# Twelve columns of the second gate formed during the first feed-forward part, with the contraction on the partitions

## The chip, the cores and the metric

The kernel runs on one core of one Trainium2 chip. The metric is device microseconds (us) of one execution; the figure of a kernel is the median of several runs. The core has engines that each work through their own instructions in order: PE (matrix products), DVE (VectorE, elementwise work and reductions), ACT (ScalarE, copies and activations), POOL (GpSimd, here only an issuer of transfers) and SP (SyncE, the main issuer of transfers). Transfers between the chip's memory (HBM) and the on-chip memory (SBUF) run on 16 DMA engines that all queues share.

## The reference, cut to what matters

One decoder layer, 512 tokens of width 2048, everything in float32:

```python
mod_all = silu(c) @ w_ada + b_ada               # w_ada: 2048 x 12288
sh1, sc1, g1, sh2, sc2, g2 = split(mod_all, 6)  # six vectors of 2048
h = rms_norm(x, norm1_g) * (1 + sc1) + sh1
u = h @ w_in                                    # all projections
mixed = [rms_norm(conv(u)), rms_norm(attention(u))]
x = x + g1 * (mixed @ w_out)
h = rms_norm(x, norm2_g) * (1 + sc2) + sh2
x = x + g2 * (relu(h @ w_ff1) ** 2 @ w_ff2)
return rms_norm(x, normf_g)
```

The change concerns g2, the second gate. It is needed only when the second feed-forward product is added to x, which is late in the kernel. Its 2048 numbers are kept as 16 columns of 128 (one column is 128 numbers, one on each SBUF partition), columns 80 to 95 of a tile called mod. One column costs 1 MB of w_ada; the twelve of the change cost 12 MB.

## The kernel before, in words

A matrix product in float32 is made of three products of a faster type (fp32r): each operand is split into a high half (a copy on ACT) and a low half (a subtraction on DVE). The pairs are called wh and wl in the projection and at the attention's output, hl, kw, sg or gt in the feed-forward part, and tk for tokens. So each weight block of 512 KB costs a transfer, an ACT operation and a DVE operation of 128x1024 before PE can use all of it.

The kernel has three stages, and each is recorded first and then emitted by a planner (the class Order). The planner knows a cost for every operation, simulates the engines and the DMA engines, and writes out for every engine an order, in which the engine then works whatever really happens. At each point it takes the operation that could start earliest; among those that could start equally early, the one with the earliest due time, which is counted back from the PE work that needs it. For a transfer it reckons that the data move no sooner than 1.5 us after the issue, at 340 GB/s, and have landed 1.1 us after that (in Order.plan: `wire = max(wire, at + 1.5) + x.size / Order.RATE` and `end = wire + 1.1`). The projection and the attention stage are planned six times and the best plan is taken; the feed-forward stage is planned once.

The stages are these.

- **Projection.** The columns of mod are formed beside it. One column is formed by two transfers of 512 KB (wa) and two "dots" on DVE: a multiply-and-sum of 1024 products along the free dimension for each of 128 partitions, against a copy of silu(c) spread over all partitions (cs). The profile names a dot CUSTOM_DVE t<-wa,cs. The list `todo` holds the columns that are formed here, in the order g1, sc2 and sh2, and then the first of g2; `more_ada(1)` takes one at a time.
- **Attention**, with the output product of the convolution half (out_conv, blocks w_oc) as filling work. At its end, `late_ada(NATT, 4, nc.gpsimd)` forms eight columns of g2 with loads on POOL's queue, into four tiles used in turn, with dots against a copy of cs that is loaded again. Behind it stand the first two blocks of w_oa (wh, wl).
- **Feed-forward.** First the rest of the attention's output product: `late_ada(len(behind), 4, nc.sync)` forms the last four columns of g2, six more blocks of w_oa are split (hl), and then blocks of w_oa2 (kw and others). Then the first feed-forward part: `part(n)` and `results_of(p)` for the rounds p = 0 and 1, and `ff1(p)` for p = 2 to 31. A round loads four blocks of w_ff1 into a ring of six tiles (rw), forms two sums (sg) and seven split operands, and runs seven products of 24 matmuls (a Strassen scheme, named B1, U6, T5, B2, T7, B3, T4); its results are split and stored (g). Up to p = 28, two of the sums of a round are made by transfers that add (POOL's queue, w_f into rw and sg). The second feed-forward part reads them back, and uses g2 from its sixth pass on.

The tile `spare` (128x1024, called snap in the profile) holds first results of rounds 0 and 1 and is then idle until the second feed-forward part.

Because one helper records all operations, every row of the profile has the same line, L142; tiles tell the operations apart.

Of the kernel before, what the change touches and what calls it, by code (L numbers as in the profile page):

```python
# [12 lines left out]
AF = mybir.ActivationFunctionType  # L13
OP = mybir.AluOpType
AX = mybir.AxisListType

P = 128
T = 512
D = 2048
NK = D // P  # L20
# [11 lines left out]
NSIDE = 7  # L32
NWA = 8
NBANK = 6
NLATE = 12
NATT = 8
NWARM = 3
SLACK = 4.0
FAST = 378e3
# [1 line left out]
V_BADA, V_N1, V_CW, V_CB, V_GC, V_GA, V_N2, V_NF, V_C, V_ID, V_END = \  # L41
    0, 96, 112, 136, 144, 152, 160, 176, 192, 208, 336
C_COS, C_SIN, C_MASK, C_CMASK, C_ROW, C_END = 0, 512, 1024, 1152, 1280, 1281
M_SH1, M_SC1, M_G1, M_SH2, M_SC2, M_G2 = range(6)
W_A, W_F, W_V = 64, 128, 134


def weave(ap, m):

    names = " ".join("xyz"[:len(ap.shape) - 2])  # L50
    return ap.rearrange(f"p {names} (a b i) -> p {names} a i b", b=2, i=m)


def plainly(ap, m):
    names = " ".join("xyz"[:len(ap.shape) - 2])
    return ap.rearrange(f"p {names} (a i b) -> p {names} a i b", b=2, i=m)
# [256 lines left out]
def hybrid_layer(ctx: ExitStack, tc: tile.TileContext, a, out):  # L313
    nc = tc.nc
# [10 lines left out]
    def slot(dtype=F32, name="m"):  # L325
        return mainp.tile([P, SLOT], dtype, name=name, tag="m")
# [5 lines left out]
    nc = order = Order(tc, xs[0].tensor.tag, NMAIN, passes=6)  # L332
# [63 lines left out]
    vec = consts.tile([P, V_END], F32, name="vec")  # L396
# [15 lines left out]
    ones = consts.tile([P, P], F32, name="ones")  # L412
# [3 lines left out]
    mod = consts.tile([P, 96], F32, name="mod")  # L416
# [4 lines left out]
    sc = small.tile([P, NK], F32, name="sc", bufs=1)  # L421
# [37 lines left out]
                             start=True, stop=True)  # L459
        return row_bcast(bank, total[:, t0:t1], width, dst[:, t0 * P:t1 * P])  # L460

    def row_bcast(bank, total, width, dst, turned=False):
        n = total.shape[-1]
        rs = small.tile([P, NQ], F32, name="rs", bufs=3)[:, :n]
        nc.scalar.activation(rs, total, AF.Sqrt, scale=1.0 / width, bias=eps)
        nc.vector.reciprocal(rs, rs)
        ps = spread(bank, rs)
        if turned:
            nc.scalar.activation(plainly(dst, W_A), weave(ps[:, :n * P], W_A), AF.Copy)
        elif dst is not None:  # L470
            nc.scalar.activation(dst, ps[:, :n * P], AF.Copy)
        return ps

# [30 lines left out]
    total = bank()  # L504
# [30 lines left out]
    for i in range(4):  # L535
# [6 lines left out]
    part = {}  # L542
    todo = [M_G1 * NK + k for k in range(NK)] + [w * NK + k for k in range(NK) for w in (M_SC2, M_SH2)] \
        + [M_G2 * NK + k for k in range(NK - NLATE)]
    behind = [M_G2 * NK + k for k in range(NK - NLATE, NK)]
    rb = accum("rb")

    def tokens(k, r):
# [98 lines left out]
    w = weights(a["w_kv"][0])  # L647
# [72 lines left out]
    def other():  # L720
        return next(others)

    def late_ada(n, slots, queue):
        c2 = [pair(name="cs") for _ in range(2)]
        for i in range(2):
            nc.sync.dma_start(out=c2[i], in_=csd[i])
        wa = [slot(name="wa")[:, :1024] for _ in range(slots)]
        for k in range(n):
            m, acc = behind.pop(0), next(accs)
            for i in range(2):  # L730
                w = wa[(2 * k + i) % slots]
                queue.dma_start(out=w, in_=a["w_ada"][2 * m + i])
                dot(w, i, acc, m, c2, temp(name="dot").bitcast(BF16))

    def more_ada(n):
# [432 lines left out]
    while m < NK:  # L1168
        out_conv(m)
        m += 1  # L1170
    late_ada(NATT, 4, nc.gpsimd)
    oa = [weights(a["w_oa"][k]) for k in range(2)]
    order.emit()
    att.close()
# [77 lines left out]

    late_ada(len(behind), 4, nc.sync)
    x1d = [dram.tile([P, 2, 2, HT], F32, name=f"x1d{i}") for i in range(NK // 2)]
    sacc = accum()
    pm = [bankf() for _ in range(8)]
# [132 lines left out]
    def outcome(p, x, y, zv):  # L1391

        store = nc.sync if p >= 30 else nc.gpsimd
        z, v = zv
        sub(z[:, 0], x[:, 0], y[:, 1])
        sub(z[:, 1], y[:, 1], y[:, 0])
        sub(v[:, 0], z[:, 0], y[:, 0], OP.add)
        sub(v[:, 1], x[:, 1], v[:, 0])
        for src, idx in ((x, (B1, B2)), (z, (T5, T7)), (v, (U6, T4))):
            g = next(gt)  # L1400
            tsplit(g, src)
            for j in range(2):
                store.dma_start(out=gd[p // 4][idx[j]][p % 4 // 2][:, p % 2].bitcast(F32), in_=g[:, j].bitcast(F32))
        for j, dst in enumerate((gd[p // 4][B3], g12d) if p >= 28 else (gd[p // 4][B3],)):
            g = temp((P, 2, HT), F32R, name="g12") if j else next(gb)
            split(g, y[:, j])
            store.dma_start(out=dst[p % 4 // 2][:, p % 2].bitcast(F32), in_=g.bitcast(F32))
# [45 lines left out]
    stay = {8: 5, 9: 6, 10: 7, 12: 1, 13: 3}  # L1453
    made, results, firsts = {}, {}, {}
    spare = slot(name="snap")[:, :1024]

    def make(n):
        p, b = plan[n][:2]
# [9 lines left out]
    def results_of(p):  # L1468
        x, y, z, v = [temp((P, 2, HT)) for _ in range(4)]
        for u in range(2):  # L1470
            nc.scalar.activation(x[:, u], results[p, u][:, LO], AF.Relu)
            sub(y[:, 1 - u], firsts[p, u], results[p, u][:, HI], OP.add)
        nc.scalar.activation(x, x, AF.Square)
        nc.scalar.activation(y, y, AF.Relu)
        nc.scalar.activation(y, y, AF.Square)
        outcome(p, x, y, (z, v))

    def part(n):
        p, b, i, u, hf, first = plan[n]
# [23 lines left out]
            results_of({13: 1, 15: 0}[n])  # L1503
    for p in range(NP, 32):
        ff1(p)


    ngate = consts.tile([P, NK], F32, name="ngate")
# [186 lines left out]
def _layouts(np, x, c, w_ada, b_ada, norm1_g, w_in, conv_w, conv_b, cmp_pe_k, cmp_pe_v, cmp_w1_k,  # L1695
# [16 lines left out]
    xt = x[0].T.reshape(NK // 2, 2, P, T).transpose(0, 2, 1, 3)  # L1712
    d["xt"] = xt.reshape(NK // 2, P, 2, T // P, P)[..., _stored(np, W_A)].reshape(xt.shape)
    d["xr"] = xt.reshape(NK // 2, P, 2, 2, T // 2)[..., _in_turn(np, W_F)].reshape(xt.shape)
    d["w_ada"] = w_ada[0].T.reshape(96, P, 2, 1024).transpose(0, 2, 1, 3).reshape(192, P, 1024)
    d["vec"] = np.concatenate(
        [cols(b_ada), cols(norm1_g), cols(conv_w), cols(conv_b), cols(gnorm_conv_g), cols(gnorm_attn_g),
         cols(norm2_g), cols(normf_g), c[0].reshape(NK, P).T, np.eye(P, dtype=np.float32), cmp_pe_k[0].T, cmp_pe_v[0].T, cmp_w2_k[0][:P], cmp_w2_k[0][P:],
# [47 lines left out]
```

## Time and profile before

| | |
|---|---|
| runs | 2025.38, 2024.46, 2023.94 us; median 2024.46 |
| profiled execution, its own time | 2025.47 us |
| its span, first to last instruction | 2023.7 us |
| mean granted clock of PE | 0.991 |
| busy: PE, DVE, ACT, POOL | 98%, 89%, 51%, 9% of the span |
| projection, attention, feed-forward (by PE's first s and first pf matmul) | up to 510, up to 688, up to 2024 us |

How to read it: a row of a timeline has the start, the duration, the engine, the operation, the tile written and the tiles read, and the shape; "x3" means three merged operations, and a bracket holds the idle time of the engine just before and what ended it. A group row has the count, then the busy time in us and the mean in ns, then idle time. In the list of transfers stand the count, the size and the median time from issue to landing. "PE" is the matrix engine's matmuls, "PEld" the loading of its weights.

### The profile page before, as it was taken

Reading aid. Unit: us, or ns where it says so; the run is one execution under the profiler, and the core shown is the slowest. Engines: PE = TensorE matmul, PEld = TensorE weight load, DVE = VectorE, ACT = ScalarE, POOL = GpSimd, SP = SyncE. Lnnn points to the kernel's source line nnn. Section 1 sums busy time; section 2 is a strip of 40 time slices with the busy share of each in tenths; the row PEclk is TensorE's granted clock in tenths of the full one; section 3 lists DMA queues with packets and bytes.
Section 4 is the critical chain, followed back from the end, with each engine's and each line's share of the span. In section 5 each row is a group of like instructions: output and inputs, shape, how many; then the busy total and the mean of one; then the engine's idle time right before and its main releaser. Section 6 shows DMA issues by size and latency. Waiting matters only on the chain.

```text
span 2023.7 us, 37782 instructions
## 1 busy us (share of the span) xinstructions
PE 1979.9 (98%) x14930; PEld 1887.1 (93%) x14930; DVE 1799.1 (89%) x2639; ACT 1036.4 (51%) x1533; POOL 182.9 (9%) x304
## 2 busy tenths in 40 slices
PE   8999999999999889999999999999999999999997
PEld 6888888989888779999999999999999999999997
DVE  8999988888998777988888888888989999999998
ACT  5444343334677236766666666665543333344345
POOL 0000000000000100233223223211000000000010
PEclk9999999999999989999999999999999999999999
DMA  9897688886211873698898899878867457468572
GB/s 374 333 353 251 231 290 315 288 302 243 93 63 63 284 274 129 178 296 257 271 281 253 264 280 261 257 232 315 298 226 262 152 212 271 157 214 294 181 233 100
DMA packets 140929, 487.19 MB, mean 241 GB/s; under 512 B 16976, under 2 KB 21584, under 8 KB 140752
## 3 DMA queue, kind: packets, MB, share of 16 engines
q1 hardware_dynamic: 111056, 384.10, 52.6%
q0 software_dynamic: 29120, 99.63, 18.4%
q8 instruction: 117, 1.92, 0.4%
q10 hardware_dynamic: 576, 1.05, 0.1%
q14 instruction: 60, 0.49, 0.1%
HBM read 415.51 MB, written 69.21 MB: 240 GB/s over the span
## 4 chain that ended last, share of the span: by engine, by line
PE 83%; DVE 9%; DMA 4%; issue 2%; ACT 1%; DVEq 0%; SPq 0%; ACTq 0%; POOLq 0%
PE pf L142 56%; PE ps L142 21%; PE pw L142 2%; DVE hl L142 2%; DVE xt L142 2%; PE s L142 2%; DMA wa<-in_w_ada 2%; PE pv L142 1%; DVE t L142 1%; PE pt L142 1%; DVE sg L142 1%; DMA rw<-in_w_f 1%; DVE wl L142 1%; DMA raw<-in_cmp_w 1%; DMA sg<-in_w_f 0%
## 5 line engine op out<-in xcount | busy, mean ns | idle before, releaser
L142 PE MATMUL pf<-tk,hl 128*128 128x256 f32 x10656 | 1193.9, 275 | 5.1 <-DVE t L142 2.6
L142 PEld LDWEIGHTS pf<-tk,hl 128*128 128x128 f32 x10656 | 1191.5, 192 | 6.6 <-issue 4.3
L142 ACT ACTIVATE hl<-rw 128x1024 fp32r<-128x1024 f32 x264 | 280.5, 1062 | 334.3 <-PE pf L142 309.6
L142 DVE TENSOR_TENSOR hl<-rw,hl 128x1024 fp32r<-128x1024 f32 x264 | 322.9, 1224 | 43.2 <-ACT hl L142 42.9
L142 ACT ACTIVATE hl<-sg 128x1024 fp32r<-128x1024 f32 x183 | 194.7, 1065 | 222.2 <-PE pf L142 199.5
L142 ACT ACTIVATE wh<-raw 128x1024 fp32r<-128x1024 f32 (+1 forms) x106 | 112.3, 1060 | 227.2 <-PE ps L142 170.4
L142 DVE TENSOR_TENSOR hl<-sg,hl 128x1024 fp32r<-128x1024 f32 x153 | 187.3, 1226 | 31.8 <-ACT hl L142 30.8
L142 PE MATMUL ps<-h_m,wh 128*128 128x512 f32 x720 | 215.0, 380 | 0.0
L142 PE MATMUL ps<-h,wh 128*128 128x512 f32 x560 | 166.0, 383 | 3.4 <-ACT h L142 2.6
L142 PEld LDWEIGHTS ps<-h_m,wh 128*128 128x128 f32 x720 | 135.2, 189 | 18.5 <-DVE h_m L142 0.2
L142 DVE TENSOR_TENSOR wl<-raw,wh 128x1024 fp32r<-128x1024 f32 (+1 forms) x106 | 129.9, 1226 | 16.6 <-ACT wh L142 15.5
L142 DVE CUSTOM_DVE_ANT_0 t<-wa,cs,acc 128x1024 bf16<-128x1024 f32 x96 | 123.1, 1283 | 23.6 <-DMA wa<-in_w_ada 22.3
L142 DVE CUSTOM_DVE_ANT_0 t<-wa,cs,vec 128x1024 bf16<-128x1024 f32 x96 | 122.9, 1282 | 17.1 <-DMA wa<-in_w_ada 16.5
L142 PE MATMUL ps<-h_m,wl 128*128 128x512 f32 x360 | 136.8, 380 | 0.0
L142 PEld LDWEIGHTS ps<-h,wh 128*128 128x128 f32 x560 | 106.3, 191 | 20.3 <-ACT h L142 4.2
L142 DVE TENSOR_TENSOR sg<-sg,rw 128x1024 f32<-128x1024 f32 x92 | 112.7, 1225 | 2.1
L142 POOL DMA_DIRECT2D g<-gt x180 | 97.0, 550 | 119.0 <-issue 55.2
L142 PE MATMUL ps<-h,wl 128*128 128x512 f32 x280 | 103.2, 381 | 0.0
L142 DVE TENSOR_TENSOR xt<-xt,pf 128x512 f32<-128x512 f32 x128 | 85.8, 683 | 9.4 <-PE pf L142 9.2
L142 POOL DMA_DIRECT2D rw<-in_w_f x30 | 26.3, 876 | 658.3 <-DVE sg L142 658.3
L142 PE MATMUL pw<-mix,wh 128*128 128x512 f32 x256 | 82.2, 392 | 0.0
L142 PEld LDWEIGHTS ps<-h_m,wl 128*128 128x128 f32 x360 | 68.2, 189 | 9.2
(240 smaller groups left out, 2282.1 us busy)
## 6 DMA issues: line engine op xcount, KB each, us to landing
rw<-in_w_f SPq DMA_DIRECT2D x260, 512.0 KB, 4.8
wa<-in_w_ada SPq DMA_DIRECT2D x176, 512.0 KB, 6.4
tk<-g SPq DMA_DIRECT2D x114, 512.0 KB, 6.5
g<-gt POOLq DMA_DIRECT2D x180, 256.0 KB, 7.1
raw<-in_w_conv SPq DMA_DIRECT2D x32, 512.0 KB, 4.5
rw<-in_w_f POOLq DMA_DIRECT2D x30, 512.0 KB, 6.1
sg<-in_w_f POOLq DMA_DIRECT2D x30, 512.0 KB, 5.5
raw<-in_w_kv SPq DMA_DIRECT2D x16, 512.0 KB, 6.4
```

Of the source, the lines that this page charges most:

```text
L142: x.i, x.eng, x.call = len(self.nodes), eng, (lambda: real(*args, **kw))
```

## The change

All sixteen columns of g2 leave the projection's list. Four (the first) are formed by `late_ada` at the start of the feed-forward stage, as four were before. The other twelve are formed in another way during the first feed-forward part, and the call at the attention's end is gone.

The new way: w_ada's last 1536 columns are laid out as `w_gate`, 48 blocks of 256 KB in which the contraction index lies on the partitions. `gate_part(s)` loads block s into the first half of `spare` and runs two DVE operations of 128x256 on it: each multiplies 256 outputs by one column of silu(c) (sc) as a scalar per partition, and adds to a running sum gsum in the last quarter of `spare`. After eight blocks, sixteen columns of sc have been used, and two matmuls with a column of ones sum gsum over the partitions; one small DVE operation adds the bias and writes two columns of mod. So two columns of g2 take eight blocks, and twelve take 48. The loop over p calls two blocks a round from p = 3 to p = 26. There is one tile for the loads, so a load waits until both operations on the block before are done. The rest of the diff drops an argument of row_bcast that no call uses.

```diff
-NLATE = 12
-NATT = 8
+NLATE = 16
+NGATE = 12
...
-    behind = [M_G2 * NK + k for k in range(NK - NLATE, NK)]
+    behind = [M_G2 * NK + k for k in range(NK - NLATE, NK - NGATE)]
...
-    def late_ada(n, slots, queue):
+    def late_ada(n, slots):
...
-                queue.dma_start(out=w, in_=a["w_ada"][2 * m + i])
+                nc.sync.dma_start(out=w, in_=a["w_ada"][2 * m + i])
...
-    late_ada(NATT, 4, nc.gpsimd)
     oa = [weights(a["w_oa"][k]) for k in range(2)]
...
-    late_ada(len(behind), 4, nc.sync)
+    late_ada(len(behind), 4)
...
     spare = slot(name="snap")[:, :1024]
+    gsum = spare[:, 3 * HT:]
...
+    def gate_part(s):
+
+        n, b = s // 8, s % 8
+        nc.sync.dma_start(out=spare[:, :T], in_=a["w_gate"][s])
+        for j in range(2):
+            w, c = spare[:, j * HT:(j + 1) * HT], sc[:, 2 * b + j:2 * b + j + 1]
+            if b + j == 0:
+                nc.vector.tensor_scalar(gsum, w, c, None, op0=OP.mult)
+            else:
+                nc.vector.scalar_tensor_tensor(out=gsum, in0=w, scalar=c, in1=gsum, op0=OP.mult, op1=OP.add)
+        if b == 7:
+            total = bankf()
+            m = M_G2 * NK + NK - NGATE + 2 * n
+            with floating():
+                for i in range(2):
+                    nc.tensor.matmul(total[:, i:i + 1], gsum[:, i * P:(i + 1) * P], ones[:, 0:1], start=True, stop=True)
+                nc.vector.tensor_tensor(out=mod[:, m:m + 2], in0=total[:, :2],
+                                        in1=vec[:, V_BADA + m:V_BADA + m + 2], op=OP.add)
...
     for p in range(NP, 32):
         ff1(p)
+        for s in range(2 * (p - NP - 1), 2 * (p - NP)):
+            if 0 <= s < 4 * NGATE:
+                gate_part(s)
...
+    early = D * 6 - P * NGATE
+    d["w_ada"] = w_ada[0][:, :early].T.reshape(-1, P, 2, 1024).transpose(0, 2, 1, 3).reshape(-1, P, 1024)
+    d["w_gate"] = w_ada[0][:, early:].reshape(8, 2, P, -1, T // 2).transpose(3, 0, 2, 1, 4).reshape(-1, P, T)
```

More of the change, by code (lines that the diff above doesn't have):

```diff
@@ L460, in row_norm, with row_bcast @@
         return row_bcast(bank, total[:, t0:t1], width, dst[:, t0 * P:t1 * P])
-    def row_bcast(bank, total, width, dst, turned=False):
+    def row_bcast(bank, total, width, dst):
         n = total.shape[-1]
@@ L467, in row_bcast @@
         ps = spread(bank, rs)
-        if turned:
-            nc.scalar.activation(plainly(dst, W_A), weave(ps[:, :n * P], W_A), AF.Copy)
-        elif dst is not None:
+        if dst is not None:
             nc.scalar.activation(dst, ps[:, :n * P], AF.Copy)
@@ L1714, in _layouts @@
     d["xr"] = xt.reshape(NK // 2, P, 2, 2, T // 2)[..., _in_turn(np, W_F)].reshape(xt.shape)
-    d["w_ada"] = w_ada[0].T.reshape(96, P, 2, 1024).transpose(0, 2, 1, 3).reshape(192, P, 1024)
+    early = D * 6 - P * NGATE
+    d["w_ada"] = w_ada[0][:, :early].T.reshape(-1, P, 2, 1024).transpose(0, 2, 1, 3).reshape(-1, P, 1024)
+    d["w_gate"] = w_ada[0][:, early:].reshape(8, 2, P, -1, T // 2).transpose(3, 0, 2, 1, 4).reshape(-1, P, T)
     d["vec"] = np.concatenate(
```

## The prediction

> **What bounds the kernel now.** The page comes first: how much of the span the matrix engine (PE) is busy, and which chain of work ended last.
>
> ```profile
> span 2023.7 us, 37782 instructions
> PE 1979.9 (98%) x14930; PEld 1887.1 (93%) x14930; DVE 1799.1 (89%) x2639; ACT 1036.4 (51%) x1533; POOL 182.9 (9%) x304
> PE 83%; DVE 9%; DMA 4%; issue 2%; ACT 1%; DVEq 0%; SPq 0%; ACTq 0%; POOLq 0%
> ```
>
> PE is the bound: 43.8 us (2023.7 - 1979.9) are all the time in which it does nothing. So an edit pays only by taking some of those 43.8 us away, or by shortening matmuls that run at a low clock, and it costs where it makes PE wait or adds to PE. The profiled execution took 2025.47 us, 1.8 us more than its span and 1.0 us more than the median of the runs (2024.46). I make the sum against 2025.5 and take 1.0 off at the end.
>
> The second view is PE's own timeline, read for its gaps near the places that the change touches: the end of the projection, and the border between attention and feed-forward part.
>
> ```profile
> 511.68 0.90 PE L142 MATMUL s<-kslc,q 128*128 128x160 f32 x6 [1.46 <-ACT gates L142]
> 516.00 0.56 PE L142 MATMUL s<-kslc,q 128*128 128x160 f32 x3 [2.52 <-DVE pc L142]
> 687.74 0.59 PE L142 MATMUL pf<-mixa,wh 128*128 128x512 f32 x2
> 692.79 0.38 PE L142 MATMUL pf<-mixa,wh 128*128 128x512 f32 x1
> 693.01 0.38 PE L142 MATMUL pf<-mixa,wl 128*128 128x512 f32 x1
> 696.49 0.48 PE L142 MATMUL pf<-mixa,wl 128*128 128x512 f32 x1 [2.67 <-DVE wl L142]
> 715.39 5.06 PE L142 MATMUL pf<-mixa,hl 128*128 128x512 f32 x11 [11.77 <-DVE hl L142]
> ```
>
> The bracket is the idle time ahead of a group and what ended it. The border holds 2.67 + 11.77 = 14.44 us of the 43.8, the start of attention another 1.46 + 2.52 = 3.98. Who makes PE wait stands in the timelines of VectorE (DVE) and ScalarE (ACT) at that border:
>
> ```profile
> 687.73 1.06 ACT L142 ACTIVATE wh<-raw 128x1024 fp32r<-128x1024 f32 x1 [4.61 <-PE pw L142]
> 688.69 1.04 ACT L142 ACTIVATE hl<-rw 128x1024 fp32r<-128x1024 f32 x1
> 688.52 1.28 DVE L142 CUSTOM_DVE_ANT_0 t<-wa,cs,acc 128x1024 bf16<-128x1024 f32 x1 [3.89 <-DMA wa<-in_w_ada]
> 695.21 1.22 DVE L142 TENSOR_TENSOR wl<-raw,wh 128x1024 fp32r<-128x1024 f32 x1
> 696.46 7.74 DMA rw<-in_w_oa
> 712.90 1.28 DVE L142 CUSTOM_DVE_ANT_0 t<-wa,cs,acc 128x1024 bf16<-128x1024 f32 x1 [7.55 <-DMA wa<-in_w_ada]
> 714.11 3.49 DVE L142 TENSOR_TENSOR hl<-rw,hl 128x1024 fp32r<-128x1024 f32 x3
> ```
>
> The operations t<-wa,cs are the "dots" of the second gate, and DVE works in order. The high half of the second w_oa block (wh) is ready at 688.8, but its low half (wl) stands behind five dots and starts at 695.21: PE waits 2.67 us. The next three low halves (hl) stand behind the sixteenth dot, whose weights land at 712.9: PE waits 11.77 us. All sixteen belong to the call at the attention's end, which the change takes out.
>
> **The change part by part.**
>
> *Taken out at the border: sixteen dots, sixteen loads on POOL's queue, two loads of cs on SP's.* Beside the two gaps goes the low clock behind them:
>
> ```profile
> 690.00:700.00 10.00, 7.30 (x28) 5.50 (x27) 8.93 (x14) 0.00 (x0) 2.63 (x5) 0.88 0.77 251
> 700.00:710.00 10.00, 3.62 (x15) 2.76 (x13) 2.59 (x4) 2.11 (x2) 0.53 (x1) 0.84 1.02 415
> 710.00:720.00 10.00, 4.61 (x11) 3.67 (x12) 7.06 (x8) 0.00 (x0) 0.00 (x0) 0.50 0.61 221
> 720.00:730.00 10.00, 10.00 (x45) 8.64 (x44) 1.92 (x4) 2.69 (x3) 0.00 (x0) 0.93 0.75 286
> ```
>
> Columns are PE, weight load, DVE, ACT and POOL busy, then granted clock, DMA share and GB/s. Busy time times the missing clock: 7.30 x 0.12 + 3.62 x 0.16 + 4.61 x 0.50 + 10 x 0.07 = 4.5 us. Gaps and clock are 14.4 + 4.5 = 18.9 us. (The Trainium skill, TensorE: Matmul & The Clock Gate, "What's actually happening", has the clock halved after an idle window of about 3.4 us. By it the gap of 2.67 us would cost no clock, and this term would be about 1.5 us smaller. The windows show a clock of 0.88 and 0.84 behind that gap, so the trace disagrees and decides.)
>
> What is late next there? Without the dots wl can end at 688.8 + 1.2 = 690.0. The loads of the fourth and later w_oa blocks, which follow wl, then start near 690 in place of 696.46; with the same 7.7 us they land at 697.7, and ACT (1.06) and DVE (about 1.2) make them ready at 700. PE, from 687.74 with 24 matmuls per block at 0.22 us (692.79 to 693.01), 5.3 us a block, wants the fourth at 703.6: 3.6 us to spare. The four columns that stay behind have their loads on SP behind these six. I take the whole 18.9; the low end is 7, if a load or one of the eight dots that stay takes the place of the large gap.
>
> *Taken out in the projection: four columns, eight dots and eight loads.* They are the last ones in the queue there:
>
> ```profile
> 491.50 1.28 DVE L142 CUSTOM_DVE_ANT_0 t<-wa,cs,acc 128x1024 bf16<-128x1024 f32 x1
> ...
> 496.91 1.29 DVE L142 CUSTOM_DVE_ANT_0 t<-wa,cs,acc 128x1024 bf16<-128x1024 f32 x1
> 512.13 2.51 DVE L142 SCALAR_TENSOR_TENSOR q<-t,q 128x512 fp32r<-128x512 f32 x4
> 515.00:520.00 5.00, 4.00 (x16) 3.29 (x17) 3.94 (x22) 3.01 (x12) 0.00 (x0) 0.66 0.07 25
> 520.00:525.00 5.00, 5.00 (x23) 4.40 (x24) 2.85 (x12) 2.09 (x8) 0.00 (x0) 0.66 0.00 0
> ```
>
> DVE runs without a pause into the first attention block and ends its q at 514.6; three of the eight dots, 3.9 us, lie in that run. Taking them out brings attention's start forward by up to 3.9 us, and up to 9.00 x 0.34 = 3.1 us of clock with it: 7.0 at most. The whole projection and attention are ordered anew by the planner, which can lose what it wins; I put the low end at -3, as much as the smaller of these terms. I take 4.0, the two gaps.
>
> *Added to PE: twelve column sums, each a matmul of 128x1 in f32.* The trace has this form:
>
> ```profile
> 384.23 1.05 PE L142 MATMUL ps<-ones,sacc 128*128 128x1 f32 x8 [0.70 <-DVE sacc L142]
> 385.14 0.36 PE L142 MATMUL ps<-wh,h 128*128 128x268 f32 x1
> L142 PE MATMUL pf<-ones,sacc 128*128 128x1 f32 x16 | 2.2, 243 | 0.2 <-DVE sacc L142 0.2
> ```
>
> Four of them hold PE from 384.23 to 385.14, 0.23 us each: 12 x 0.23 = 2.7 us. The other group gives 0.14 per record, 1.7 us, as the low end. PE has no gap in that stage (next fence), so this is paid in full.
>
> *Added to DVE and the DMA engines in the first feed-forward part: 48 loads of 256 KB on SP's queue, and behind each two operations of 128x256.* The twenty-four rounds p = 3 to 26, on which they are spread, take 450 us:
>
> ```profile
> 882.00:1332.00 450.00, 450.00 (x4032) 450.00 (x4031) 389.29 (x531) 290.72 (x410) 133.16 (x216) 1.00 0.90 268
> 1350.00:1400.00 50.00, 50.00 (x450) 50.00 (x449) 47.33 (x64) 29.82 (x43) 7.50 (x14) 1.00 0.74 254
> L142 DVE TENSOR_TENSOR t<-t 128x256 f32<-128x256 f32 x95 | 40.0, 421 | 0.0
> L142 DVE SCALAR_TENSOR_TENSOR x<-pf,mod,x 128x256 f32<-128x256 f32 x16 | 7.3, 480 | 6.1 <-PE pf L142 6.1
> rw<-in_w_f SPq DMA_DIRECT2D x96, 512.0 KB, 6.0
> g<-gb POOLq DMA_DIRECT2D x24, 256.0 KB, 5.3
> x<-in_xr SPq DMA_DIRECT2D x15, 256.0 KB, 4.5
> ```
>
> A round is 450 / 24 = 18.75 us. DVE is busy 389.29 / 24 = 16.22 of them and idle 2.53. Two steps a round are four operations of 0.42 us, 1.68: 0.85 us is left (0.61 if an operation takes 0.48). DVE would be at 95%, and in 1350 to 1400 it is at 47.33 of 50 beside a PE at 50.00, so the work by itself is hidden. The DMA engines are idle for 0.10 x 450 = 45 us; 48 x 0.262 MB at the 415 GB/s that they reach in 700 to 710 are 30 us. That fits too, if closely.
>
> What is not hidden by this is waiting. There is one tile, so a load waits for DVE's second operation on the load before, and DVE's next operation waits for the landing with every hl of the stage queued behind it. SP's weight loads stand behind the gate's load, but are issued well ahead. The planner reckons a 256 KB load at 1.5 + 0.77 + 1.1 = 3.4 us (constants in its code) and places DVE's operation from then on. The nearest rows say 4.5 us (same queue and size, quiet engines), 5.3 (same size, this stage, POOL's queue) and 6.0 (same queue and stage, twice the size). DVE's waits come in one cluster a round; here are the first and the last wait over 0.3 us of one round and the first of the next:
>
> ```profile
> 1020.56 0.42 DVE L142 TENSOR_TENSOR t<-pf,t 128x256 f32<-128x256 f32 x1 [0.43 <-PE pf L142]
> ...
> 1024.27 1.23 DVE L142 TENSOR_TENSOR hl<-sg,hl 128x1024 fp32r<-128x1024 f32 x1 [0.61 <-ACT hl L142]
> ...
> 1039.32 0.42 DVE L142 TENSOR_TENSOR t<-pf,t 128x256 f32<-128x256 f32 x1 [0.42 <-PE pf L142]
> ```
>
> The gate's operations come last in due time and so fall into these 4 us; one load of the two is then met tightly, and the other lands during the long busy stretch. With 4.5 us the wait is 1.1, less the free 0.85: 0.25 us x 24 = 6 us. With 3.4 it is 0; with 6.0, 2.6 - 0.85 = 1.75 x 24 = 42 us. I take the 4.5 row because size and queue are those of the gate's load.
>
> Sum: 2025.5 - 18.9 - 4.0 + 2.7 + 6 = 2011.3 for a profiled execution, **2010 us** for the median.
>
> **The rivals.**
>
> *The gate's loads land late all through the first feed-forward part, and DVE becomes the bound.* Place: rounds 3 to 26. With a landing of 5.5 us, between the rows of this stage, a round costs 16.22 + 1.68 + 2.1 = 20.0 us in place of 18.75, and 24 rounds 30 us: 2025.5 - 22.9 + 2.7 + 30 = 2035, median 2034, slower than before. It decides from the landing at which 24 x (wait - 0.85) exceeds the 20.2 us won, a wait of 1.7 us, a landing of 5.1. For it speaks a DMA share of 0.90 in that stage; against it that the dots of the projection, which meet the same planner in a busy stage, wait seldom:
>
> ```profile
> DVE t L142 <- DMA wa<-in_w_ada: 18.9, 17, 2.3
> ```
>
> That is 18.9 us in 17 waits between 200 and 500 us, the longest 2.3, though those loads have four tiles and the gate's has one. (The Trainium skill, DMA: Bandwidth & Descriptors, "Issuing engines are not separate DMA queues", speaks for this rival: transfers of SP and POOL share the same sixteen engines, so moving the loads from POOL's queue to SP's buys no room.)
>
> *The first feed-forward part hides everything.* The 256 KB loads land by the time that the planner reckons, or DVE comes late to each: the 6 us fall away, 2004 us. For it speaks that the planner gives the gate's operations the latest due time, so that any other ready operation goes first. (The Trainium skill, same page, "Anatomy of one DMA", puts a transfer at 2.0 us plus its bytes at 436 GB/s, an estimate of 2.6 us for 256 KB: by it every load is in time. The quiet 4.5 us row disagrees.)
>
> *The border keeps half its gap.* The eight dots that stay, or the loads of w_oa, hold the low halves up: the gain there is 7 to 12, the time 2017 to 2022. For it speaks that the dots that stay are ordered among the same hl operations; against it the 3.6 us to spare worked out above.
>
> **How the numbers follow.** Forecast (2006 to 2015) 0.45; all hidden (2000 to 2006) 0.17; half the gap stays (2015 to 2022) 0.18; DVE bound in the first feed-forward part (2022 to 2045) 0.20. The likeliest case's own range is 2006 to 2015. To leave out no more than 2 in 10, about one on each side, the range is 2001 to 2033: the low end has 7.0 from attention's start and nothing lost later, the high end nearly the price of the first rival. About 0.2% (4 us) is what a measurement of this kernel tells from no change, so faster means below 2020.4 and slower above 2028.5: faster 0.45 + 0.17 + 0.13 = 0.75; same 0.05 + 0.05 = 0.10; slower 0.15.
>
> **What would show it.** Border: no gap over 1 us on PE from its first pf matmul for 30 us, a granted clock of 1.00 there, and PE's first tk,hl matmul about 23 us earlier. Attention's start: no wait of s for DVE pc. First feed-forward part: DVE at 95% or a little more, waits of DVE for the load of w_gate of about 1 us once a round, a round of 19.0 us or less. Rounds of 19.6 us or more would make the prediction wrong; so would an hl that waits at the border for w_oa or w_ada.

## The result, and the profile after

The changed kernel takes 2042.85 us (median of 5 runs, 2036.48 to 2049.36) beside 2023.94 us (2022.89 to 2025.38) for the kernel before on the same chip. The ratio is 1.0095, with a 95% interval of 1.0068 to 1.0122. The change makes the kernel slower by 19 us where the forecast had it 14 us faster. The profiled execution took 2042.85 us, its span is 2041.0.

First the page of the changed kernel: span, busy times, the shares of the chain that ended last, and the last of the issues, the gate's loads.

```profile
span 2041.0 us, 37931 instructions
PE 1987.8 (97%) x14954; PEld 1893.1 (93%) x14954; DVE 1800.7 (88%) x2693; ACT 1034.3 (51%) x1533; POOL 175.2 (9%) x288
PE 76%; DVE 11%; DMA 8%; issue 3%; ACT 1%; DVEq 0%; SPq 0%; POOL 0%; ACTq 0%; POOLq 0%
snap<-in_w_gate SPq DMA_DIRECT2D x48, 256.0 KB, 4.9
```

PE's share of the chain has fallen from 83% to 76%, and that of the DMA engines has risen from 4% to 8%. PE's idle time is 2041.0 - 1987.8 = 53.2 us, 9.4 more than before. The rest of the 17.3 us between the spans is PE work: some at a low clock, some added.

PE's timeline from the end of the projection to the border, and a window of the border:

```profile
509.78 1.28 PE L142 MATMUL s<-kslc,q 128*128 128x160 f32 x9
680.59 0.60 PE L142 MATMUL pf<-mixa,wh 128*128 128x512 f32 x2
690.95 39.28 PE L142 MATMUL pf<-mixa,hl 128*128 128x512 f32 x216
690.00:700.00 10.00, 10.00 (x48) 8.76 (x47) 3.28 (x5) 1.06 (x1) 0.00 (x0) 1.00 1.03 417
765.91 2.84 PE L142 MATMUL pf<-tk,hl 128*128 128x256 f32 x24
```

The border does what was forecast: 216 matmuls of the low and high halves in one group without a bracket, the clock at 1.00, and the first tk,hl matmul at 765.91. In the trace of before it stands at 792.98, so 27.1 us are won by there: 687.74 - 680.59 = 7.1 by the first pf matmul, and 20.0 at the border.

All of that, and more, is lost again in the first feed-forward part. Its windows, and the waits between 800 and 1450 us:

```profile
820.00:1360.00 540.00, 513.91 (x4490) 508.87 (x4489) 460.96 (x691) 317.90 (x452) 147.92 (x239) 0.99 0.91 269
DVE snap L142 <- DMA snap<-in_w_gate: 39.8, 21, 4.5
PE pf L142 <- DVE snap L142: 16.0, 6, 4.5
PE pf L142 <- DVE t L142: 5.2, 8, 1.9
PE pf L142 <- DVE hl L142: 4.5, 6, 1.5
```

PE stands for 540 - 513.91 = 26.1 us. The same stretch of before has 0.7 us of that:

```profile
820.00:1360.00 540.00, 539.31 (x4830) 539.15 (x4829) 472.55 (x648) 348.28 (x496) 154.98 (x252) 1.00 0.88 261
```

In the changed kernel DVE is at 460.96 of 540, 85%: it isn't the bound, it waits too. Sixteen of the 26 us are six waits of PE for snap. They are these, in PE's timeline:

```profile
924.76 0.61 PE L142 MATMUL pf<-ones,snap 128*128 128x1 f32 x4 [2.47 <-DVE snap L142]
1028.47 0.61 PE L142 MATMUL pf<-ones,snap 128*128 128x1 f32 x4 [2.32 <-DVE snap L142]
1108.91 1.01 PE L142 MATMUL pf<-ones,snap 128*128 128x1 f32 x4 [4.52 <-DVE snap L142]
1190.85 0.61 PE L142 MATMUL pf<-ones,snap 128*128 128x1 f32 x4 [4.08 <-DVE snap L142]
1277.21 0.61 PE L142 MATMUL pf<-ones,snap 128*128 128x1 f32 x4 [1.64 <-DVE snap L142]
1355.78 0.60 PE L142 MATMUL pf<-ones,snap 128*128 128x1 f32 x4 [0.94 <-DVE snap L142]
```

These are the six column sums, one for each group of eight steps. PE works in order, so everything behind a sum waits with it. The last four intervals between sums are 80.4, 81.9, 86.4 and 78.6 us, mean 81.8; the four rounds in which eight steps were to fit are 4 x 18.75 = 75.0. In PE's order 672, 672, 702 and 647 matmuls pf<-tk,hl stand in them, and four rounds are 672: the 6.8 us on top are what PE loses in a group on average, the sum itself included. One sum from close by, in the queue of SP, in DVE and in windows of 2 us behind it:

```profile
1098.80 0.33 SPq L142 DMA_DIRECT2D snap<-in_w_gate  x1
1106.84 0.48 DVE L142 SCALAR_TENSOR_TENSOR snap<-snap,sc 128x256 f32<-128x256 f32 x1 [3.06 <-DMA snap<-in_w_gate]
1107.24 1.22 DVE L142 TENSOR_TENSOR hl<-rw,hl 128x1024 fp32r<-128x1024 f32 x1
1108.38 0.48 DVE L142 SCALAR_TENSOR_TENSOR snap<-snap,sc 128x256 f32<-128x256 f32 x1
1122.86 0.34 DVE L142 TENSOR_SCALAR snap<-snap,sc 128x256 f32<-128x256 f32 x1
1108.00:1110.00 2.00, 1.09 (x5) 1.09 (x6) 1.83 (x5) 0.17 (x1) 0.01 (x1) 0.50 0.25 82
1110.00:1112.00 2.00, 2.00 (x10) 2.00 (x11) 1.98 (x4) 1.51 (x3) 0.97 (x2) 0.50 0.94 336
1112.00:1114.00 2.00, 2.00 (x14) 2.00 (x13) 0.03 (x1) 0.00 (x0) 1.55 (x3) 0.66 0.90 191
```

The load of the group's last step is issued at 1098.80, when the tile comes free, and lands 8 us later. DVE stands for 3.06 us of that with an hl behind it. The second operation on the tile stands behind that hl and ends at 1108.86, and only then can the sum run: PE has stood for 4.52 us. Then the clock is at 0.50 to 0.66 for some 5 us, which costs 1.09 x 0.50 + 2.00 x 0.50 + 2.00 x 0.34 = 2.2 us more, part of it in the slow sum itself. So a wait of 4.5 us is a loss of about 7. The next group's first operation comes only at 1122.86, 14.0 us behind the sum, and its last one ends 68 us later; together these are the 82 us.

The next table goes through the loss. Its numbers are worked out from PE's timelines: the start of the k-th pf<-tk,hl matmul in a kernel less its start in the trace of before (168 of these are a round; k = 0 is the start of the first feed-forward part, k = 9576 lies in the second). "Lost" is the difference of these two. The experiments named stand in the next section.

| k | 0 | 840 | 1344 | 2688 | 4032 | 5208 | 9576 | lost | end of span |
|---|---|---|---|---|---|---|---|---|---|
| changed kernel | -27.1 | -24.4 | -16.0 | -12.9 | +1.4 | +13.7 | +15.6 | 42.7 | +17.3 |
| e1_no_gate | -26.9 | -26.4 | -26.4 | -26.4 | -26.4 | -26.4 | -26.4 | 0.5 | -25.9 |
| e2_one_load | -25.2 | -25.2 | -23.5 | -22.4 | -21.3 | -20.8 | -20.8 | 4.4 | -19.6 |
| e3_small_ops | -28.4 | -27.3 | -17.5 | -15.6 | -5.7 | +11.0 | +11.0 | 39.4 | +13.7 |
| e4_three_tiles | -26.3 | -25.5 | -20.9 | -19.8 | -18.8 | -18.3 | -18.4 | 7.9 | -16.0 |
| e5_late_sum | -27.0 | -26.6 | -22.1 | -10.8 | +11.5 | +36.9 | +36.8 | 63.8 | +38.6 |
| e6_later_ops | -26.0 | -26.0 | -26.0 | -6.9 | +13.8 | +34.9 | +34.9 | 60.9 | +32.9 |
| e9_sum_later_two_sums | -27.3 | -25.6 | -14.3 | -13.7 | +2.2 | +8.9 | +22.0 | 49.3 | +23.2 |
| e10_half_rate | -22.0 | -21.9 | -16.7 | -15.8 | -15.4 | -14.9 | -14.8 | 7.2 | -12.5 |
| e11_three_tiles_reckoned | -24.8 | -24.6 | -23.6 | -23.1 | -21.8 | -10.7 | -10.7 | 14.1 | -10.1 |
| e12_three_tiles_later | -24.5 | -23.9 | -22.1 | -21.6 | -20.5 | -20.0 | -19.6 | 4.9 | -17.3 |

### The profile page after: what moved, and what is told of

It reads as the page before. It is cut to its first block, busy times and chain, and to the rows that moved or that the text cites. A ratio compares the mean times of both kernels' runs of the same rounds, so it can differ in the third digit from the quotient of the medians.

```text
span 2041.0 us, 37931 instructions
## 1 busy us (share of the span) xinstructions
PE 1987.8 (97%) x14954; PEld 1893.1 (93%) x14954; DVE 1800.7 (88%) x2693; ACT 1034.3 (51%) x1533; POOL 175.2 (9%) x288
## 4 chain that ended last, share of the span: by engine, by line
PE 76%; DVE 11%; DMA 8%; issue 3%; ACT 1%; DVEq 0%; SPq 0%; POOL 0%; ACTq 0%; POOLq 0%
PE pf L142 48%; PE ps L142 21%; DMA snap<-in_w_gate 4%; PE pw L142 4%; DVE hl L142 3%; DVE xt L142 2%; DVE t L142 2%; PE s L142 1%; PE pv L142 1%; DMA wa<-in_w_ada 1%; DVE sg L142 1%; DVE snap L142 1%; PE pt L142 1%; DMA g<-gt 1%; DMA raw<-in_cmp_w 1%
## 5 line engine op out<-in xcount | busy, mean ns | idle before, releaser
L142 PE MATMUL pf<-tk,hl 128*128 128x256 f32 x10656 | 1207.2, 276 | 18.0 <-DVE t L142 6.7
L142 PEld LDWEIGHTS pf<-tk,hl 128*128 128x128 f32 x10656 | 1200.4, 193 | 22.8 <-issue 12.9
L142 DVE TENSOR_TENSOR hl<-rw,hl 128x1024 fp32r<-128x1024 f32 x264 | 322.5, 1222 | 26.4 <-ACT hl L142 25.9
L142 DVE TENSOR_TENSOR wl<-raw,wh 128x1024 fp32r<-128x1024 f32 (+1 forms) x106 | 130.3, 1229 | 21.7 <-ACT wh L142 20.8
L142 DVE CUSTOM_DVE_ANT_0 t<-wa,cs,vec 128x1024 bf16<-128x1024 f32 x84 | 107.9, 1284 | 16.9 <-DMA wa<-in_w_ada 16.0
L142 DVE CUSTOM_DVE_ANT_0 t<-wa,cs,acc 128x1024 bf16<-128x1024 f32 x84 | 108.0, 1285 | 9.8 <-DMA wa<-in_w_ada 9.2
L142 ACT ACTIVATE t<-t 128x512 f32<-128x512 f32 (+3 forms) x132 | 74.1, 569 | 50.3 <-DVE t L142 48.6
```

The costliest lines, as they stand in the source:

```text
L142: x.i, x.eng, x.call = len(self.nodes), eng, (lambda: real(*args, **kw))
```

## The experiments

All are edits of the changed kernel. Each time is a median, and each ratio is against the kernel before on the same chip (2023.3 to 2024.3 us there). The theory to begin with: the loss comes from the serial chain through the one load tile, whose lateness reaches PE at each column sum. The rivals: DVE's added work, the transfers as such, or waits of DVE that would cost the same however the sums stand.

**The twelve columns left out.**

```diff
 def gate_part(s):
-    (the whole body)
+    if s == 0:
+        m = M_G2 * NK + NK - NGATE
+        nc.vector.tensor_copy(mod[:, m:m + NGATE], vec[:, V_BADA + m:V_BADA + m + NGATE])
```

> Left out: the forming of the twelve columns; they are set to the bias by one small copy. Everything else is as in the changed kernel. At the same PE work the changed kernel's trace stands 27.1 us ahead of the one before when round 3 of the first feed-forward part begins, and 13.6 us behind when round 30 does. If the whole loss belongs to the gate's steps (all three theories: waiting for the loads, DVE's added work, crowding of the transfers), this kernel takes 2024 - 27 = 1997 us, give or take 4. If the loss has another root (the reordered feed-forward stage, something left behind by the attention), it stays at 2030 or more.

Measured: 1999.35 us, ratio 0.9875 (0.9859 to 0.9892). The loss of the first feed-forward part is gone (0.5 us in the table), so all of it comes from the steps of gate_part, and the two gains ahead of it are whole.

**One load in place of 48**, all operations and sums kept:

```diff
-        nc.sync.dma_start(out=spare[:, :T], in_=a["w_gate"][s])
+        if s == 0:
+            nc.sync.dma_start(out=spare[:, :T], in_=a["w_gate"][s])
```

> Left out: 47 of the 48 loads of w_gate; all 96 DVE operations and the twelve column sums stay, on the first block's data. Waiting (the loads land later than the planner reckons, and DVE and then PE, each in order, stand still): 1997 + 3 for the sums = 2000, give or take 5. Crowding (12.6 MB more among the transfers): the same, 2000. DVE's added work (95% of a round): the loss stays, 2035 to 2045.

Measured: 2005.41 us, ratio 0.9909 (0.9894 to 0.9924), 0.4 us above the range of waiting and crowding and 30 below that of DVE's work. The stretch 820 to 1320 us of the kernel without the columns, and of this one:

```profile
820.00:1320.00 500.00, 499.18 (x4467) 498.75 (x4466) 433.22 (x593) 320.99 (x454) 149.29 (x243) 1.00 0.90 269
```

```profile
820.00:1320.00 500.00, 498.36 (x4457) 497.86 (x4456) 463.64 (x692) 318.67 (x450) 149.45 (x244) 1.00 0.91 268
```

The operations bring DVE from 433.22 to 463.64 us, 93%, and PE keeps 498.36 of 500. DVE's work is hidden, and it doesn't bound this part.

**Small operations**, 2 columns wide but for the first of each group; loads, tile and sums stay, the formed columns are left out but for their first parts:

```diff
-            w, c = spare[:, j * HT:(j + 1) * HT], sc[:, 2 * b + j:2 * b + j + 1]
+            w, c = spare[:, j * HT:j * HT + 2], sc[:, 2 * b + j:2 * b + j + 1]
...
-                nc.vector.scalar_tensor_tensor(out=gsum, in0=w, scalar=c, in1=gsum, op0=OP.mult, op1=OP.add)
+                nc.vector.scalar_tensor_tensor(out=gsum[:, :2], in0=w, scalar=c, in1=gsum[:, :2], op0=OP.mult, op1=OP.add)
```

> Left out: most of the products; each gate operation but the first of a group works on 2 columns in place of 256, so it costs DVE 0.1 us and not 0.48. All 48 loads, their one tile and the sums on PE stay, and so does every wait. Waiting: most of the loss stays, 2030 to 2045. DVE's added work: the loss goes, 2000 to 2006. Crowding: it stays, 2035 to 2045.

Measured: 2034.15 us, ratio 1.0052 (1.0036 to 1.0069). Its waits between 800 and 1450 us:

```profile
DVE snap L142 <- DMA snap<-in_w_gate: 39.8, 19, 3.8
PE pf L142 <- DVE snap L142: 15.5, 7, 4.1
```

With the work taken out and the loads left, both waits stay as they were (39.8 and 16.0). It is the loads and their chain.

**Three load tiles in turn**, with the same 48 loads, operations and sums:

```diff
-        nc.sync.dma_start(out=spare[:, :T], in_=a["w_gate"][s])
+        hold = (spare[:, :T], sacc, r2)[s % 3]
+        nc.sync.dma_start(out=hold, in_=a["w_gate"][s])
...
-            w, c = spare[:, j * HT:(j + 1) * HT], sc[:, 2 * b + j:2 * b + j + 1]
+            w, c = hold[:, j * HT:(j + 1) * HT], sc[:, 2 * b + j:2 * b + j + 1]
```

> Nothing is left out. The loads go in turn into three tiles (the idle one and two that held row sums and factors of the norm, which nothing uses at that time), so a load is issued two steps ahead. Waiting: the waits of DVE for w_gate fall from 39.8 us to under 10, 2000 to 2010. DVE's added work or crowding: no change against the changed kernel, 2035 to 2045.

Measured: 2008.53 us, ratio 0.992 (0.9905 to 0.9935), faster than both kernels. The same stretch, PE's wait for snap, and the loads:

```profile
820.00:1320.00 500.00, 496.77 (x4425) 496.14 (x4424) 460.62 (x688) 317.13 (x448) 148.34 (x241) 1.00 0.96 289
PE pf L142 <- DVE snap L142: 2.2, 1, 2.2
sacc<-in_w_gate SPq DMA_DIRECT2D x32, 256.0 KB, 5.2
```

The DMA engines are busier (0.96, against 0.92 in this stretch of the changed kernel) and a load takes about as long (5.2 us for two of the tiles and 4.7 for the third, against 4.9), but DVE's waits for the loads are down from 39.8 to 1.2 us, and PE's for snap to 2.2 us in one. So it is neither the traffic nor the landing time by itself. What hurts is that a load can't start before both operations on the one before are done.

**The sums planned 8 us later**, one load tile (the bias add that writes mod has no delay of its own; it can only follow the sum):

```diff
             with floating():
+                order.slack = 8.0
                 for i in range(2):
                     nc.tensor.matmul(total[:, i:i + 1], ...)
+                order.slack = 0.0
                 nc.vector.tensor_tensor(out=mod[:, m:m + 2], ...)
```

> The changed kernel, with the twelve column sums alone planned 8 us after the planner takes the group's running sum to be ready; operations, loads and the one tile as they are. In the changed kernel PE stood still 16.0 us in six waits for that running sum. If PE, in order, loses its time at the sums, those 16 us come back: 2027, give or take 4. If the sums only show a delay that the hl operations behind DVE's waits would bring anyway, the time stays at 2036 to 2046.

Measured: 2067.08 us, ratio 1.0221 (1.0195 to 1.0246). Both expectations missed. PE no longer waits for snap, but for mod; the waits, and one of them in PE's timeline:

```profile
PE pf L142 <- DVE mod L142: 31.4, 5, 7.4
1025.88 0.50 PE L142 MATMUL pf<-ones,snap 128*128 128x1 f32 x4
1033.78 8.44 PE L142 MATMUL pf<-tk,hl 128*128 128x256 f32 x51 [7.40 <-DVE mod L142]
```

No product of this part reads the twelve columns of mod. By the code, what ties a tk,hl matmul to that operation is the PSUM bank: the sums take one from the same ring of eight (`bankf()`), and its next user must wait until mod has been written from it. So a sum has a deadline, the eighth taking of a bank behind its own. The trace agrees: the five waits stand four rounds apart, ahead of the tk,hl matmuls k = 2160, 2832, 3504, 4176 and 4848. Put off to that deadline, as here, a sum makes PE stand until the bias add is done. At 1025.88 that took 7.1 us behind the sum's end, since nine other operations come first in DVE's order.

**The first operation of each step planned 4 us behind the reckoned landing**, one load tile:

```diff
         for j in range(2):
...
+            order.slack = 4.0 if j == 0 else 0.0
...
+        order.slack = 0.0
```

> The changed kernel, with the first of the two DVE operations of each step planned 4 us after the landing that the planner reckons (7.4 us after the issue instead of 3.4); same instructions, same tile. If the planner's short reckoning is the cause, DVE's waits for w_gate fall from 39.8 us to under 10 and the time to 2003 to 2012. If one tile is the cause whatever the reckoning (the chain of eight steps is then longer than the four rounds that it has), waits move to PE, and the time stays above 2025.

Measured: 2059.2 us, ratio 1.0179 (1.016 to 1.0197). The waits, and the last three sums in PE's timeline:

```profile
PE pf L142 <- DVE snap L142: 41.5, 5, 14.7
DVE snap L142 <- DMA snap<-in_w_gate: 4.1, 1, 4.1
1207.35 1.01 PE L142 MATMUL pf<-ones,snap 128*128 128x1 f32 x4 [6.46 <-DVE snap L142]
1292.94 1.01 PE L142 MATMUL pf<-ones,snap 128*128 128x1 f32 x4 [6.66 <-DVE snap L142]
1378.98 1.01 PE L142 MATMUL pf<-ones,snap 128*128 128x1 f32 x4 [7.24 <-DVE snap L142]
```

The second theory held. DVE hardly waits for a load any more (4.1 us in one wait, 39.8 in 21 without the edit), and the kernel is slower than ever but one. The waits moved from DVE to PE. Sums come 85.6 and 86.0 us apart, against 75.0 for four rounds, and each group loses those 10.6 to 11.0 us; 60.9 are lost in all. All five waits end in a sum at the places where its bank is due (k = 2160, 2832, 3504, 4176 and 4848). So DVE's waits for the loads are no measure of the loss; how late the chain ends is. The edit plans the first operation 7.4 us behind the issue, where a load of the changed kernel takes 4.9 in the median, so it lengthens the chain itself. What a plan with about 5 us and one tile would do wasn't run.

**Three tiles, and two banks passed over** ahead of the second feed-forward part, for a loss near the end that is told of below:

```diff
(three load tiles, and behind the loop over p)
+    for _ in range(8 - NGATE // 2):
+        bankf()
```

> The kernel with three tiles, and two more turns of the ring of eight PSUM banks before the second feed-forward part, so that the six banks taken by the column sums and these two make one full turn. The kernels with sums lose 3.5 us near the end (PE waits for DVE xt, 2.3 us the longest), the one without the gate does not. If the shifted turn of the banks is the cause, 2008.5 - 3.5 = 2005, and that wait is below 1 us. If the cause is anything else of the gate, it stays at 2008.5, give or take 1.5.

Measured: 2007.77 us, ratio 0.9926 (0.9909 to 0.9943). No change against three tiles alone; a shifted turn of the banks isn't the cause.

**The four columns put back into the projection** (NLATE = 12, no call of late_ada at the start of the feed-forward stage), the twelve left out:

```diff
-NLATE = 16
+NLATE = 12
...
-    late_ada(len(behind), 4)
```

> The kernel without the twelve columns, with the first four columns of the gate formed in the projection again (as before the change) and none at the feed-forward part's start. If the gain of 7 us that the changed kernel shows at its first pf matmul comes from taking these four out of the projection, that matmul comes at 687 to 688 again and the time is 1999.4 + 7 = 2006. If it comes from the attention's end being planned anew without its dots, it stays at 681 and the time is 1999 or less.

Measured: 2005.64 us, ratio 0.9913 (0.9896 to 0.9931), against 1999.35 without the four. Its first pf matmul stands at 686.37 (680.59 in the changed kernel). So taking four columns out of the projection is worth about 6 us, more than the 4.0 of the forecast.

**Two running sums in turn, and each sum recorded three rounds later**, one load tile:

```diff
-        if b == 7:
+            gsum = spare[:, (2 + n % 2) * HT:(3 + n % 2) * HT]
...
+        if b == 5 and n:
+            n -= 1
...
-            if 0 <= s < 4 * NGATE:
+            if 0 <= s < 4 * NGATE + 6:
```

> Edit: the loads still share one tile, but two running sums of 256 columns take turns, and the column sums of a group with their PSUM bank are recorded three rounds later, in the middle of the next group. All twelve columns are formed. Theory 1 (the deadline: VectorE may wait for the loads, but PE stands still only because each column sum has to come right at the end of its own eight steps): PE's waits ahead of the sums (16.0 us in 6) go, VectorE's waits for w_gate stay near 40 us, the first feed-forward part loses under 12 us, time 2006 to 2014. Theory 2 (VectorE's waits for the loads hold up the low halves themselves, and the sums only show it): the time stays at 2030 or more, with PE waiting for hl, t or snap in the same stretches.

Measured: 2048.34 us, ratio 1.0114 (1.0095 to 1.0132). The time is that of theory 2, and so are PE's waits: those ahead of the sums stay (16.8 us in 4). DVE's waits for the loads stay as well (37.3 us), as theory 1 had it. The second, the fourth and the sixth sum in PE's timeline:

```profile
1062.62 0.61 PE L142 MATMUL pf<-ones,snap 128*128 128x1 f32 x4
...
1246.87 1.02 PE L142 MATMUL pf<-ones,snap 128*128 128x1 f32 x4 [4.50 <-DVE snap L142]
...
1422.31 1.01 PE L142 MATMUL pf<-ones,snap 128*128 128x1 f32 x4 [7.15 <-DVE snap L142]
```

The second group used up the later deadline (no wait at 1062.62), and from then on the sums stand at the end of their groups as before, (1422.31 - 1062.62) / 4 = 90 us apart. Moving the deadline once gives a chain that is too slow a single delay and no more. So the run went as theory 2 said, but it doesn't rule out theory 1, since the later deadline gave room to one group only.

**Half the rate**: one step a round, six of the twelve columns, one load tile:

```diff
-        for s in range(2 * (p - NP - 1), 2 * (p - NP)):
-            if 0 <= s < 4 * NGATE:
+        for s in range(p - NP - 1, p - NP):
+            if 0 <= s < 2 * NGATE:
```

> Edit: one step a round in place of two, through the same one tile; six of the twelve columns are formed, the other six are left out (they get the bias alone). Theory 1 (a chain of eight serial steps of 8 to 12 us has to fit into the rounds of its group: 64 to 96 us against four rounds of 75 us do not, against eight rounds of 150 us do): no wait of PE over 1 us ahead of the three sums, time 2000 to 2006. Theory 2 (each load costs a fixed part of the loss, 40.8 us / 48 = 0.85 us): half of the loss stays, about 20 us, time 2018 to 2026.

Measured: 2011.15 us, ratio 0.9934 (0.9919 to 0.9949), 5 us above theory 1's range and 7 below theory 2's. All of its sums in PE's timeline, and the waits:

```profile
954.08 0.61 PE L142 MATMUL pf<-ones,snap 128*128 128x1 f32 x4
1104.48 0.51 PE L142 MATMUL pf<-ones,snap 128*128 128x1 f32 x4
1255.01 0.51 PE L142 MATMUL pf<-ones,snap 128*128 128x1 f32 x4
DVE snap L142 <- DMA snap<-in_w_gate: 10.8, 4, 5.0
PE pf L142 <- DVE hl L142: 2.0, 1, 2.0
```

No sum waits, and they come 150.4 and 150.5 us apart, which is eight rounds: PE sets the pace, not the chain. What the mechanism foretold is there. The loss is 7.2 us where half of 42.7 would be 21.4; 5.2 of it fall between k = 840 and 1344, where DVE waits 5.0 us for one load and PE 2.0 for the hl behind it. In the profiled execution (2012.98 us) another 5 us came before: PE's lead at k = 0 is 22.0 us in place of 27.1, and the first s matmul stands at 514.85 in place of 509.78, though the two kernels' DVE and ACT work through the same operations in the same order until 480 us. That is a spread of executions in the projection; how much of the median's 5 us it explains isn't shown.

**Three tiles, and the first operation planned 2 us later**; **three tiles, and the steps begun three rounds later**:

```diff
+            order.slack = 2.0 if j == 0 else 0.0
```

```diff
-        for s in range(2 * (p - NP - 1), 2 * (p - NP)):
+        for s in range(2 * (p - NP - 4), 2 * (p - NP - 3)):
```

> Edit: the three load tiles of the earlier experiment, and the planner puts the first operation of each step 2 us behind the landing that it reckons (3.4 + 2.0 = 5.4 us, what these loads take there). All twelve columns are formed. Theory 1 (once the chain through one tile is broken, what is left in the first feed-forward part is loads met too early): the 2.2 us of PE ahead of the first sum and the 4.4 us that are lost around it go, time 2001 to 2005. Theory 2 (that loss comes from the crowded DMA engines of the first six rounds, DMA share 0.96 to 0.99, whatever is reckoned): 2006 to 2011, as with three tiles alone.

> Edit: the three load tiles, with the 48 steps begun three rounds later (rounds 6 to 29 in place of 3 to 26). All twelve columns are formed. Theory 1 (loads met too early wherever they stand): the loss of about 5 us moves to a later place, time 2006 to 2011. Theory 2 (the first rounds are crowded by what is left of the attention's weights and tokens): the loss goes, 2001 to 2006, and with it the wait of PE ahead of the first sum.

Measured: 2012.98 us, ratio 0.9952 (0.9937 to 0.9967), and 2006.55 us, ratio 0.9912 (0.9889 to 0.9935). The first is above both theories' ranges. In it the loss around the first sum is gone, and a new one stands at the fifth:

```profile
1256.57 1.01 PE L142 MATMUL pf<-ones,snap 128*128 128x1 f32 x4 [4.89 <-DVE snap L142]
```

There the plan begins the group 38 us after the group before has ended, and runs into the sum's deadline (k = 4176); neither theory had that. In the second, the operations of the first group still run from 832 us on, since the planner takes what is ready, and only the sum has moved:

```profile
887.14 0.99 DVE L142 SCALAR_TENSOR_TENSOR snap<-sacc,sc,snap 128x256 f32<-128x256 f32 x2
929.01 0.60 PE L142 MATMUL pf<-ones,snap 128*128 128x1 f32 x4
```

The last operation ends at 888.13 and the sum follows 41 us later, without a wait, and no sum of this kernel has one. Its time lies in theory 1's range and just above theory 2's, while the wait ahead of the first sum is gone, as theory 2 had it. Both spoke of the loads and not of the sum, and the early loads haven't moved; what the run shows is that with room between a group's end and its sum most of the last loss there is gone (1.8 us from k = 840 to 1344, beside 4.6 with three tiles alone). Its time doesn't differ from that of three tiles alone by more than the runs spread.

## Why the prediction was wrong

**Border: right.** 18.9 us forecast, 20.0 measured; no wait, clock 1.00.

**Attention's start and the projection: right in kind, too small.** 4.0 forecast with 7.0 as the bound. The first s matmul stands where it was (509.78 and 509.76) and the two gaps behind it are gone; the lead at the first pf matmul is 7.1 us, and e8_projection_back puts the four columns at about 6 us. Executions with the same order of work up to there have their first s matmul anywhere from 508.45 (e3_small_ops) to 514.85 (e10_half_rate), so no finer split is shown.

**Column sums on PE: right.** 2.7 forecast; the kernel with one load loses 4.4 us in this part with sums and operations, most of it evenly (0.5 to 0.6 us from sum to sum). The low end of 1.7 us was misread: a matmul of this form leaves two records (the twelve sums leave 24), so 0.14 per record is 3.3 us for twelve.

**DVE's work is hidden: right.** 93% with one load and PE at 498.36 of 500.

**"What is not hidden is waiting": the step that failed.** It has each late load cost its wait less DVE's free 0.85 us, round by round, 6 us in all. With the sums, the forecast for this part was 8.7; it lost 42.7. The mechanism was wrong, not a size of it:

- The landing was taken well enough: 4.5 us, measured 4.9 in the median (2.5 at least, 8.7 at most). DVE's waits sum up to 39.8 us, 1.66 a round, and with 0.85 free the formula gives 19 us. But with the waits nearly gone (e6_later_ops) the kernel was slower still, so a price on DVE's waits is no price of this change. That the prediction's 42 us for a landing of 6.0 comes so close to the 42.7 is luck: it needs 2.6 us of waiting a round.
- The step looked at one load at a time. Eight loads through one tile are one chain: issue, landing, first operation, an hl or two of 1.22 us between, second operation, next issue. In the trace a group takes 65 to 98 us from its first operation to its last, and the next begins 6 to 21 us later. PE's order, which is the plan's, shows how tight that is. The second sum stands 887 matmuls pf<-tk,hl behind the first, where four rounds are 672, and from there the sums stand 46, 46, 46, 16 and 41 matmuls (2 to 5 us) ahead of the places where their banks are due. So with one tile the plan itself had used up the room, even at its 3.4 us a load. With three tiles the same sums stand 526, 382, 262, 262 and 404 matmuls ahead (29 to 59 us), and none of them waits; a group takes 56 to 87 us there, not much less, but the next one begins 1 to 11 us behind it.
- The prediction counted the sums as PE work, 0.23 us each, and didn't ask what they wait for. A sum is where the chain itself meets PE's queue, and in PE's order it comes due whether or not the chain is done. Of the 42.7 us, 26.1 are PE standing: 16.0 in the six waits for snap, most of the rest for low halves and results (t, hl) that come late from a DVE that waits. The clock falls to half behind three of the six waits, the first, the third and the fourth, and costs 1.6, 2.2 and 1.7 us there; the sums cost 2.8 us as matmuls. About 8 us are not resolved by these views.

The first rival had the place, and with 2034 us the nearest time, for another reason: it makes DVE the bound at 20.0 us a round. DVE is at 85%, and between the sums the changed kernel has rounds of 18.76 us. What would have shown the real one before the result: the eight steps added up as a chain. With the 5.3 us row, a load, two operations of 0.42, an hl of 1.23 between them and SP's next issue of 0.33 come to 7.7 us, 62 of the 75 us, if DVE comes to each at once. That leaves 1.7 us a step for a DVE that is busy nearly all the time and works in the planner's order; and the question which PE instruction stands at the chain's end has the price.

**Open.** In the last 150 us the changed kernel and the three-tile kernels lose another 3 to 5 us (e4_three_tiles: -18.4 at k = 9576, -14.9 at k = 10080), those without the columns don't. There PE waits 2.3 us for an xt that the plan puts behind an hl and an sg on DVE. That this order differs is seen; why the plan comes out so isn't. How much of a group's 82 us is landing, and how much is the plan's choice of when DVE comes to a step and when the next group begins, was not measured apart either; the pause behind a sum stays with two running sums. And no run keeps the one-tile chain and leaves out the sums, so how much of the 42.7 us would come through the low halves alone isn't shown.

## What to carry to other kernels

Work that is fed through one buffer is a serial chain: add up its whole round (issue, landing, the wait for the engine, the release) and hold the sum against the time it has, before counting how much each engine has free. Then look for the instruction on the bounding engine that ends the chain, and for what gives it a deadline, such as a PSUM bank in a ring: a 0.2 us matmul there costs whatever the chain is late, each time. A second and third buffer were worth 34 us here (2042.85 to 2008.53), and planning the same chain's operations later made it worse (2059.2).

## What the runs showed of the hardware

A short wait of PE can cost clock for several microseconds after it. Windows of the three-tile kernel around its single wait of 2.17 us:

```profile
884.00:886.00 2.00, 0.24 (x3) 0.05 (x1) 1.96 (x4) 0.00 (x0) 0.00 (x0) 1.00 0.98 309
886.00:888.00 2.00, 1.58 (x9) 1.58 (x10) 1.97 (x5) 0.00 (x0) 0.00 (x0) 0.72 1.02 403
888.00:890.00 2.00, 2.00 (x11) 2.00 (x11) 0.97 (x3) 0.97 (x2) 0.00 (x0) 0.50 1.07 415
890.00:892.00 2.00, 2.00 (x19) 2.00 (x18) 2.00 (x4) 1.67 (x4) 0.28 (x1) 0.92 0.98 392
```

The clock falls to 0.50 although PE stood for 2.17 us only, and the busy time at a low clock costs 1.58 x 0.28 + 2.00 x 0.50 + 2.00 x 0.08 = 1.6 us on top. Not every such wait does that: behind the wait of 2.32 us at 1028.47 in the changed kernel the clock stays at 1.00, and the runs don't show what decides it.

```profile
1030.00:1032.00 2.00, 2.00 (x20) 2.00 (x19) 1.73 (x4) 1.50 (x4) 1.23 (x4) 1.00 1.00 399
```

The Trainium skill, TensorE: Matmul & The Clock Gate, "What's actually happening", has the lower clock come after at least one idle window of about 3.4 us. The two values, half and full, agree with these rows; the 3.4 us don't, since 2.17 us were enough here.

Loads of 256 KB landed after 4.9 us in the median at a DMA share of 0.92 (changed kernel, 820 to 1320 us), and after 5.2 at 0.96 (two of the three tiles): the busier engines lengthened them little, and with three tiles in turn DVE waited 1.2 us for them in place of 39.8.
